# Lookup gates of the expert layer: two groups of four tokens in one run, in a fixed order between the projections

## The chip, the cores and the metric

One core of a Trainium2 chip runs the whole program. The metric is the device time in microseconds of that core, as the median over runs. The core has TensorE (PE in the rows; its weight loads are PEld), VectorE (DVE), ScalarE (ACT), GpSimd (POOL) and SyncE (SP), which issues the loads. Each engine takes its instructions in the order in which the built program lists them, and waits for the others by semaphores.

## The reference, cut to what matters

Two blocks run one after the other on 256 tokens of width 1024. The first has two layers, and each ends with `peer`, a layer that looks up 16 of 16384 experts for each token and head. The change touches that function alone, which runs twice.

```python
def peer(xn, w_q, sub_keys, u, v):
    q = (t @ w_q).reshape(n_tok, PEER_HEADS, 2, PEER_DKEY // 2)
    sc = jnp.einsum('thpd,hpnd->thpn', q, sub_keys).astype(jnp.float32)
    s1, i1 = lax.top_k(sc[:, :, 0], PEER_TOPK)
    s2, i2 = lax.top_k(sc[:, :, 1], PEER_TOPK)
...
    top_s, pos = lax.top_k(cand, PEER_TOPK)
    eidx = jnp.take_along_axis(cidx, pos, axis=-1)
    gate = jax.nn.softmax(top_s, axis=-1).astype(xn.dtype)
...
        hid = jax.nn.gelu(jnp.einsum('td,thkd->thk', tc, u[ec]), approximate=False)
        return jnp.einsum('thk,thkd->td', gc * hid, v[ec])
```

## The kernel before

The kernel does not gather experts. It computes the hidden value of all 128 x 128 experts for all tokens, multiplies it by a gate matrix that is zero where an expert is not picked, and multiplies the product by all of `peer_v`.

**Projections.** The loop over `i1` makes 128 projections, one for each first key. A projection is `acc_t`: 24 matmuls of 128x256 into the PSUM tile `ph`, 16 with the high half `whi` of a block of `peer_u` and 8 with its low half `wlo`. `wload` fetches the block into `raw`; ScalarE casts `whi`, VectorE subtracts to get `wlo` (both L98, two buffers each). ScalarE's Gelu takes `ph` to a row of H, which is three tiles: `low` (rows 0 to 63, H_2056 in the order's rows of the first layer), `mid` (64 to 95, H_1356) and `last` (96 to 127, H_1349). PSUM has two `ph` buffers.

**Routing.** Beside the first projections VectorE runs the list `steps`, which finds the experts of every token; `advance` deals some of it out after each projection. It ends with four lookups (L724 to L731) and `to_picks`, which transposes the picks on TensorE (`it`, L738) and casts them to `IT` (L744, L745). The scratch of these steps lies in `mid` and `last`.

**Gates.** Four tokens are a group, and there are 64 groups. `build` has VectorE make the rows of a group: `pab` (one 128x1024 comparison, L801) and `pgb` (two 128x512 products, L806), in two buffers each. `gates` has TensorE multiply them in 8 half-precision matmuls into the PSUM tile `g`. Then, for the rows of H that exist by then, VectorE multiplies H by `g` (L824), and for the others ScalarE copies `g` there (L826), so that a later Gelu is multiplied in (L842, L843).

**Values.** After the last projection, H is split into two halves `hw` (L98), and 128 blocks of `peer_v` are accumulated into four PSUM tiles `acc`.

**Order.** The program is written with these loops, and a scheduler places each instruction in its engine's list by what it needs. Before, the gates were tied to nothing but their data. The order in which gates and projections stand on TensorE was the scheduler's.

Of the kernel before, what the change touches and what calls it, by code (L numbers as in the profile page):

```python
# [19 lines left out]
P = 128  # L20
S = 256
D = 1024
DK = D // P
# [16 lines left out]
NO_SYNC = mybir.DependencyInfo(mybir.DependencyClass.NoSync, mybir.DependencyReason.DATA)  # L40
# [13 lines left out]
def program(tc, A, out, stop=None, start=None):  # L54
# [22 lines left out]
    def mmt(nm, side=None):  # L77
        banks[0] += 1
        return mm_ps.tile([P, 512], F32, tag=f"mm{banks[0] % 2 if side is None else side}", name=nm)

    def smt(nm="sm"):
        return sm_ps.tile([P, 512], F32, tag="sm", name=nm)
# [19 lines left out]
    def wload(src, pool=None, tag="w", raws=None, rawtag="raw", after=None, behind=None):  # L102
        raw = (raws or rawp).tile([P, 1024], F32, tag=rawtag, name="raw")
        with tc.issue_after(after) if after else nullcontext():
            loads[:] = [nc.sync.dma_start(raw, src)]
        hi = (pool or wp).tile([P, 1024], F32R, tag=tag + "hi", name=tag + "hi")
        lo = (pool or wp).tile([P, 1024], F32R, tag=tag + "lo", name=tag + "lo")
        i = split(raw, hi, lo)
        for x, y in zip(i, behind or ()):
            tc.add_manual_dep(x.ins, y.ins.name, NO_SYNC, reason="behind")  # L110
        return hi, lo
# [5 lines left out]
    def mm(o, l, r, start, stop):  # L117

        i = nc.tensor.matmul(o, l, r, start=start, stop=stop)  # L119
        per, n = paced  # L120
        if per and n // per < len(marks):
            tc.add_manual_dep(i.ins, marks[n // per].name, NO_SYNC, reason="pace")
            paced[1] += 1
        return i
# [6 lines left out]
    def acc_t(o, w, xT, base, nk, n=P):  # L131

        for a, bs in ((0, (0, 1)), (1, (0,))):
            for k in range(nk):
                ws = w[a][:, base + k * P:base + k * P + n]
                for b in bs:
                    mm(o, ws, xT[b][:, k, :], a == 0 and b == 0 and k == 0, a == 1 and k == nk - 1)

    def acc_w(o, w, x, nk, n=P):

# [32 lines left out]
    def proj_t(o, src, xT, n=P):  # L173
        acc_t(o, wload(src), xT, 0, DK, n)
# [45 lines left out]
    def xtiles():  # L220
        both = xp.tile([P, 2, DK, S], F32R, tag="x", name="x")
        x = Parts(both[:, i, :, :] for i in range(2))
        x.both = both
        return x
# [391 lines left out]
    def peer(l, xT, make):  # L616
        with ExitStack() as es:
# [3 lines left out]
            last = hbp.tile([P, 32, S], F32, tag="last", name="H")  # L621
# [47 lines left out]
            def first_level(t, c):  # L669
                def f():  # L670
                    hh, r = divmod(c, 2)
                    top16(SC[:, t, c, :], SV[:, t, hh, r, :], SI[:, t, hh, r, :], tmp)
                return 1.0, f
# [73 lines left out]
            steps = [first_level(t, c) for c in range(16) for t in range(2)]  # L747
# [6 lines left out]
            done = [0]  # L754
            credit = [0.0]

            def advance(limit, us):
                credit[0] = min(credit[0] + us, 4.0)
                while done[0] < min(limit, len(steps)) and credit[0] > 0:
                    cost, f = steps[done[0]]  # L760
                    f()
                    done[0] += 1
                    credit[0] -= cost

            def score(c):
                q = qTs[c % 2]
                ps = smt("sc")
                for t in range(2):
                    mm(ps[:, tok(t)], q[:, tok(t)], keys[:, c * P:(c + 1) * P], True, True)
                ACT.copy(SC[:, :, c, :], ps[:, :S].rearrange("p (t n) -> p t n", t=2))  # L770

            ws = [wload(A["peer_w_q"][l, c]) for c in range(2)]
            pqs = [mmt("pq") for _ in range(2)]
            acc_first(pqs, ws, xT)
            for c in range(16):
                if c > 1:
                    pq = mmt("pq")
                    acc_t(pq[:, :S], w, xT, 0, DK)
                if c > 0:
                    w = wload(A["peer_w_q"][l, c + 1] if c < 15 else A["peer_u"][l, 0])  # L780
                if c > 1:
                    ACT.copy(qTs[c % 2], pq[:, :S])
                else:
                    halves_first(qTs[c], pqs[c])
                if c > 0:
                    score(c - 1)
                advance(2 * c - 2, STEP_US)
# [3 lines left out]
            def rows(a, b):  # L791
                return next(x[:, a - o:b - o, :] for o, end, x in parts if b <= end)

            built = {}

            def build(grp):


                it = IT[:, grp].rearrange("p r t k -> p (r t) k")[:, :, None, :]
                ab = pw.tile([P, 2, 4, P], F16, tag="pab", name="pab", bufs=2)  # L800
                V.tensor_tensor(ab.rearrange("p r t (i k) -> p (r t) i k", k=2),  # L801
                                iota1.rearrange("p (i k) -> p i k", k=2)[:, None, :, :].to_broadcast([P, 8, 64, 2]),
                                it[:, 0:8].to_broadcast([P, 8, 64, 2]), op=ALU.is_equal)
                g = pw.tile([P, 4, 2, P], F16, tag="pgb", name="pgb", bufs=2)
                for r in range(2):
                    V.tensor_tensor(g[:, :, r, :].rearrange("p t (i k) -> p t i k", k=2),  # L806
                                    ab[:, 0].rearrange("p t (i k) -> p t i k", k=2),
                                    it[:, 8 + 4 * r:12 + 4 * r].to_broadcast([P, 4, 64, 2]), op=ALU.mult)
                built[grp] = ab, g

            def gates(grp, n):

                t0 = 4 * grp
                ab, g = built.pop(grp)
                ps = smt("g")
                for i in range(4):
                    for r in range(2):
                        mm(ps[:, i * P:(i + 1) * P], ab[:, 1, i, :], g[:, i, r, :], r == 0, r == 1)
                pv = ps.rearrange("p (t i) -> p i t", t=4)
                for o, end, part in parts:  # L820
                    hv = part[:, :, t0:t0 + 4]
                    m = min(max(n, o), end)
                    if m > o:
                        V.tensor_tensor(hv[:, :m - o], hv[:, :m - o], pv[:, o:m], op=ALU.mult)  # L824
                    if m < end:
                        ACT.copy(hv[:, m - o:], pv[:, m:end])  # L826

            grp, due = 0, 0.0
            for i1 in range(NK):
                ph = mmt("ph")  # L830
                acc_t(ph[:, :S], w, xT, 0, DK)
                if i1 < NK - 1:
                    w = wload(A["peer_u"][l, i1 + 1])
                if i1 == 0:
                    score(15)
                tk = 4 * grp
                hrow = rows(i1, i1 + 1)[:, 0, :]
                if tk < S:
                    ACT.activation(hrow[:, tk:], ph[:, tk:S], AF.Gelu)  # L839
                if tk > 0:  # L840
                    ge = pw.tile([P, 512], F32, tag="pw", name="ge")
                    ACT.activation(ge[:, :tk], ph[:, :tk], AF.Gelu)  # L842
                    V.tensor_tensor(hrow[:, :tk], hrow[:, :tk], ge[:, :tk], op=ALU.mult)  # L843
                if done[0] < len(steps):
                    advance(len(steps), STEP_US)
                    rate = 64.0 / (NK - 2 - i1)
                else:
                    due += rate
                    while due >= 1.0 and grp < 64:
                        if grp not in built:  # L850
                            build(grp)
                        gates(grp, i1 + 1)
                        grp += 1
                        due -= 1.0
                    if grp < 64 and grp not in built:
                        build(grp)
            while grp < 64:
                if grp not in built:
                    build(grp)
                gates(grp, NK)  # L860
                grp += 1
# [9 lines left out]
            for i1 in range(0, NK, 2):  # L871
                if i1 == 96:
# [4 lines left out]
                w = [(tail if keep else pw).tile([P, 2, S], F32R, tag=f"w{i}{i1}" if keep else "pw", name="hw")  # L877
                     for i in range(2)]
# [801 lines left out]
    else:  # L1680
        xT = xtiles()
        to_T(lambda t, k: h[:, t, k * P:(k + 1) * P], DK, lambda k, ps: split(ps, xT[0][:, k, :], xT[1][:, k, :]))
        if origin != "ln0":
# [10 lines left out]
            xT = (xT, pre, xn) if origin == "ln1" else (xT, pp, {}, ExitStack())  # L1694
# [127 lines left out]
```

## Time and profile before

| | |
|---|---|
| median of 3 runs | 2553.38 us (2549.7 to 2555.8) |
| the profiled execution | 2553.41 us, its span 2551.6 us |
| TensorE busy over the span | 2482.0 us, 97% |
| VectorE, ScalarE busy | 1894.3 us (74%), 1347.0 us (53%) |
| granted TensorE clock, mean over the span | 0.991 |

A busy TensorE counts the time between the start of a matmul and its modelled end, and neighbours overlap, so that a stretch without a gap shows as 100% busy whatever the matmuls in it are. How fast it goes there is read from the starts of the groups.

### The profile page before, as it was taken

The page shows a single profiled execution, that of the slowest core. Times are in us where ns is not written, and L with a number is a line of the kernel's source. Part 1 is how long each engine was busy: PE and PEld are TensorE (multiplying, and loading weights), DVE is VectorE, ACT ScalarE, POOL GpSimd, SP SyncE. Part 2 cuts the span into 40 slices and gives each one's busy share as a digit, 9 for nine tenths or more (in the row PEclk, how much of TensorE's full clock was granted, in tenths as well). Part 3 has the DMA queues.
Part 4 walks back from the last instruction along what each step waited for, and adds up shares of the span by engine and source line. Part 5 has one row for each costly group of instructions (what it writes and reads, how often), then busy time and mean ns, then how long its engine had stood idle before and what let it go on. Part 6 is the DMA issues. An engine that isn't in the chain of part 4 may idle for free. (4 is left out here: it accounts for less than half of the span.)

```text
span 2551.6 us, 42276 instructions
## 1 busy us (share of the span) xinstructions
PE 2482.0 (97%) x16202; PEld 2230.8 (87%) x16202; DVE 1894.3 (74%) x3669; ACT 1347.0 (53%) x2316; POOL 3.2 (0%) x24
## 2 busy tenths in 40 slices
PE   8999999999999999999999999999989999899997
PEld 7889999998888879899999998888878899688885
DVE  6679987886555567799878875555567567799997
ACT  5645555444444544556555444445464424488882
POOL 0000000000000000000000000000000000000000
PEclk9999999999999999999999999999999999999998
DMA  6535554455555554555545555556634214699993
GB/s 209 172 119 179 174 163 164 165 165 174 194 194 192 195 190 166 175 167 181 165 165 166 166 165 193 194 192 220 200 126 135 83 51 164 231 344 349 348 338 108
DMA packets 131779, 474.76 MB, mean 186 GB/s; under 512 B 15218, under 2 KB 16242, under 8 KB 131314
## 3 DMA queue, kind: packets, MB, share of 16 engines
q1 hardware_dynamic: 131570, 472.00, 54.7%
q8 instruction: 129, 2.11, 0.4%
q14 instruction: 80, 0.66, 0.1%
HBM read 470.89 MB, written 1.05 MB: 185 GB/s over the span
## 5 line engine op out<-in xcount | busy, mean ns | idle before, releaser
L98 DVE TENSOR_TENSOR wlo<-raw,whi 128x1024 fp32r<-128x1024 f32 x740 | 904.5, 1224 | 465.2 <-ACT whi L98 424.9
L98 ACT CAST whi<-raw 128x1024 fp32r<-128x1024 f32 x740 | 776.4, 1051 | 833.0 <-PE acc L119 332.6
L119 PE MATMUL ph<-x,whi 128*128 128x256 f32 x4096 | 542.5, 285 | 0.0
L119 PEld LDWEIGHTS ph<-x,whi 128*128 128x128 f32 x4096 | 508.2, 191 | 0.0
L119 PE MATMUL acc<-whi,hw 128*128 128x512 f32 x1952 | 483.7, 389 | 2.5 <-ACT hw L98 2.2
L119 PEld LDWEIGHTS acc<-whi,hw 128*128 128x128 f32 x1952 | 366.1, 188 | 79.7 <-ACT hw L98 2.6
L119 PE MATMUL ph<-x,wlo 128*128 128x256 f32 x2048 | 291.0, 284 | 0.0
L119 PEld LDWEIGHTS ph<-x,wlo 128*128 128x128 f32 x2048 | 265.4, 192 | 0.0
L119 PE MATMUL acc<-wlo,hw 128*128 128x512 f32 x976 | 261.5, 389 | 0.0
L119 PEld LDWEIGHTS acc<-wlo,hw 128*128 128x128 f32 x976 | 183.3, 188 | 38.1
L98 DVE TENSOR_TENSOR mlo<-raw,mhi 128x1024 fp32r<-128x1024 f32 x96 | 117.2, 1224 | 11.2 <-ACT mhi L98 8.3
L98 ACT CAST mhi<-raw 128x1024 fp32r<-128x1024 f32 x96 | 100.8, 1051 | 26.9 <-PE gu L119 19.7
L806 DVE TENSOR_TENSOR pgb<-pab,IT 128x512 f16<-128x512 f16 x256 | 97.0, 422 | 1.9
L839 ACT ACTIVATE H<-ph 128x256 f32<-128x256 f32 (+40 forms) x254 | 77.4, 305 | 27.3 <-PE ph L119 27.1
L801 DVE TENSOR_TENSOR pab<-iota,IT 128x1024 f16<-128x1024 f16 x128 | 87.7, 687 | 0.0
L826 ACT COPY H<-g 128x128 f32<-128x128 f32 (+20 forms) x254 | 48.2, 244 | 73.9 <-DVE H L824 73.8
L98 DVE TENSOR_TENSOR hw<-H,hw 128x512 fp32r<-128x512 f32 x128 | 87.1, 684 | 0.0
L824 DVE TENSOR_TENSOR H<-H,g 128x256 f32<-128x256 f32 (+26 forms) x254 | 71.6, 316 | 12.4 <-PE g L119 12.3
L119 PE MATMUL g<-pgb,pab 128*128 128x128 f16 x1024 | 80.8, 220 | 0.0
L98 ACT CAST hw<-H 128x512 fp32r<-128x512 f32 x128 | 77.8, 613 | 0.0
L119 PE MATMUL pq<-x,whi 128*128 128x256 f32 x512 | 73.8, 293 | 4.1 <-DVE x L302 3.2
L119 PE MATMUL gu<-whi,xc 128*128 128x512 f32 x256 | 72.6, 402 | 0.0
(635 smaller groups left out, 3121.8 us busy)
## 6 DMA issues: line engine op xcount, KB each, us to landing
raw<-in_peer_u SPq DMA_DIRECT2D x256, 512.0 KB, 3.3
raw<-in_peer_v SPq DMA_DIRECT2D x256, 512.0 KB, 4.2
raw<-in_exp_gu SPq DMA_DIRECT2D x128, 512.0 KB, 5.4
raw<-in_exp_down SPq DMA_DIRECT2D x64, 512.0 KB, 5.3
raw<-in_peer_w_q SPq DMA_DIRECT2D x32, 512.0 KB, 3.3
raw<-in_even_w_in SPq DMA_DIRECT2D x28, 512.0 KB, 4.3
raw<-in_odd_w_in SPq DMA_DIRECT2D x24, 512.0 KB, 3.4
raw<-in_w_in_g SPq DMA_DIRECT2D x16, 512.0 KB, 3.4
```

The lines of the kernel that those rows point to most:

```text
L98: return ACT.copy(hi, src), V.tensor_tensor(lo, src, hi, op=ALU.subtract)
L119: i = nc.tensor.matmul(o, l, r, start=start, stop=stop)
L801: V.tensor_tensor(ab.rearrange("p r t (i k) -> p (r t) i k", k=2), iota1.rearrange("p (i k) -> p i k", k=2)[:, None, :, :].to_broadcast([P ...
L806: V.tensor_tensor(g[:, :, r, :].rearrange("p t (i k) -> p t i k", k=2), ab[:, 0].rearrange("p t (i k) -> p t i k", k=2), it[:, 8 + 4 * r:1 ...
L824: V.tensor_tensor(hv[:, :m - o], hv[:, :m - o], pv[:, o:m], op=ALU.mult)
L826: ACT.copy(hv[:, m - o:], pv[:, m:end])
L839: ACT.activation(hrow[:, tk:], ph[:, tk:S], AF.Gelu)
```

## The change

`acc_t` returns its first and last matmul. Once the routing has ended, a chain of scheduling orders (they cost no instruction) ties each projection's last matmul, the gate matmuls that the code has behind it, and the next projection's first matmul, one behind the other. Gates are dealt out two groups at a time, whenever two are due, and after every projection the rows of the next two groups are built if they aren't yet.

```diff
@@ acc_t
-                    mm(o, ws, xT[b][:, k, :], a == 0 and b == 0 and k == 0, a == 1 and k == nk - 1)
+                    i = mm(o, ws, xT[b][:, k, :], a == 0 and b == 0 and k == 0, a == 1 and k == nk - 1)
+                    if a == 0 and b == 0 and k == 0:
+                        first = i
+        return first, i
@@ gates
+            last = [None]
...
-                        mm(ps[:, i * P:(i + 1) * P], ab[:, 1, i, :], g[:, i, r, :], r == 0, r == 1)
+                        m = mm(ps[:, i * P:(i + 1) * P], ab[:, 1, i, :], g[:, i, r, :], r == 0, r == 1)
+                        if last[0] is not None:
+                            tc.add_manual_dep(m.ins, last[0].ins.name, NO_SYNC, reason="in turn")
+                        last[0] = m
@@ the loop over i1
-                acc_t(ph[:, :S], w, xT, 0, DK)
+                i = acc_t(ph[:, :S], w, xT, 0, DK)
+                if last[0] is not None:
+                    tc.add_manual_dep(i[0].ins, last[0].ins.name, NO_SYNC, reason="in turn")
+                last[0] = i[1] if done[0] == len(steps) else None
...
-                    while due >= 1.0 and grp < 64:
-                        if grp not in built:
-                            build(grp)
-                        gates(grp, i1 + 1)
-                        grp += 1
-                        due -= 1.0
-                    if grp < 64 and grp not in built:
-                        build(grp)
+
+                    if due >= 2.0:
+                        for g in range(grp, min(grp + 2, 64)):
+                            if g not in built:
+                                build(g)
+                            gates(g, i1 + 1)
+                        grp = min(grp + 2, 64)
+                        due -= 2.0
+                    for g in range(grp, min(grp + 2, 64)):
+                        if g not in built:
+                            build(g)
```

The lines below the first edit stand 3 lower in the changed file, those below the second 9, 12 or 15 lower: L738 is L741 there, L801 is L804, L806 is L809, L824 is L833 and L843 is L855.

**TensorE, the first gates of the first layer.** `it_3205` and `it_3213` are the transposed picks of the two halves of the tokens, `ph_...` are projections in turn. Before:

```order
L119 MATMUL ph_3308<-x_1078,wlo_3286 128x256 x8
L119 MATMUL ph_3343<-x_1078,whi_3335 128x256 x16
L119 MATMUL ph_3343<-x_1078,wlo_3336 128x256 x8
L119 MATMUL ph_3396<-x_1078,whi_3370 128x256 x9
L738 MATMUL it_3205<-ident_82,H_1349 128x128 x2
L119 MATMUL ph_3396<-x_1078,whi_3370 128x256 x7
L119 MATMUL ph_3396<-x_1078,wlo_3371 128x256 x8
L119 MATMUL ph_3449<-x_1078,whi_3423 128x256 x16
L119 MATMUL ph_3484<-x_1078,whi_3476 128x256 x16
L119 MATMUL ph_3449<-x_1078,wlo_3424 128x256 x8
```

Now:

```order
L119 MATMUL ph_3295<-x_1078,wlo_3291 128x256 x8
L119 MATMUL ph_3327<-x_1078,whi_3322 128x256 x16
L119 MATMUL ph_3327<-x_1078,wlo_3323 128x256 x8
L741 MATMUL it_3205<-ident_82,H_1349 128x128 x2
L741 MATMUL it_3213<-ident_82,H_1349 128x128
L119 LDWEIGHTS pab_3253
L119 MATMUL g_3359<-pgb_3255,pab_3253 128x128
...
L119 MATMUL g_3372<-pgb_3260,pab_3258 128x128
L119 MATMUL ph_3395<-x_1078,whi_3354 128x256 x16
```

Before, 95 further projection matmuls stood between the two transposes of `it_3205` and the first gate matmul. Now the 16 matmuls of groups 0 and 1 stand right behind the transposes from which their rows are made, and the next projection stands behind all of them. From there on a run of 16 follows each third projection, up to the last run.

**VectorE, the same place.** The names are those of the routing's last steps and of the rows of groups 0 and 1. Before:

```order
L744 CAST IT_1350<-it_3205 128x32x8 x3
L98 TENSOR_TENSOR wlo_3424<-raw_3421,whi_3423 128x1024
L726 TENSOR_TENSOR H_1349<-H_1349 128x2048
L731 TENSOR_TENSOR H_1349<-H_1349 128x128
L801 TENSOR_TENSOR pab_3253<-iota1_1351,IT_1350 128x1024
L801 TENSOR_TENSOR pab_3303<-iota1_1351,IT_1350 128x1024
L98 TENSOR_TENSOR wlo_3477<-raw_3474,whi_3476 128x1024
L745 TENSOR_TENSOR IT_1350<-it_3205,IT_1350 128x32x8
L729 TENSOR_TENSOR H_1349<-H_1349 128x1024
L806 TENSOR_TENSOR pgb_3255<-pab_3253,IT_1350 128x4x128
L806 TENSOR_TENSOR pgb_3305<-pab_3303,IT_1350 128x4x128
L98 TENSOR_TENSOR wlo_3512<-raw_3509,whi_3511 128x1024
```

Now, without a row left out:

```order
L747 CAST IT_1350<-it_3205 128x32x8 x3
L732 TENSOR_TENSOR H_1349<-H_1349 128x512
L727 TENSOR_TENSOR H_1349<-H_1349 128x2048
L804 TENSOR_TENSOR pab_3253<-iota1_1351,IT_1350 128x1024
L804 TENSOR_TENSOR pab_3258<-iota1_1351,IT_1350 128x1024
L98 TENSOR_TENSOR wlo_3423<-raw_3420,whi_3422 128x1024
L748 TENSOR_TENSOR IT_1350<-it_3205,IT_1350 128x32x8
L732 TENSOR_TENSOR H_1349<-H_1349 128x256
L729 TENSOR_TENSOR H_1349<-H_1349 128x2048
L809 TENSOR_TENSOR pgb_3255<-pab_3253,IT_1350 128x4x128
L809 TENSOR_TENSOR pgb_3260<-pab_3258,IT_1350 128x4x128
L809 TENSOR_TENSOR pgb_3255<-pab_3253,IT_1350 128x4x128
```

The casts of `IT` moved ahead of the last lookups, and the rows of groups 0 and 1 still stand behind three lookup steps, a `wlo` and each other. The second layer has the same rows in the same order on both engines.

**VectorE, the end of the projections.** Before, the last gates stood one projection earlier, and only a `wlo` and one product stood ahead of the first `hw`:

```order
L824 TENSOR_TENSOR H_1349<-H_1349,g_7747 128x31x4
L843 TENSOR_TENSOR H_1349<-H_1349,ge_7744 128x252
L98 TENSOR_TENSOR wlo_7805<-raw_7802,whi_7804 128x1024
L843 TENSOR_TENSOR H_1349<-H_1349,ge_7785 128x256
L98 TENSOR_TENSOR hw_7793<-H_2056,hw_7792 128x512
```

Now the last two groups (`g_7757` and `g_7769`) come after the last projection:

```order
L98 TENSOR_TENSOR wlo_7798<-raw_7795,whi_7797 128x1024
L833 TENSOR_TENSOR H_2056<-H_2056,g_7757 128x64x4
L833 TENSOR_TENSOR H_1356<-H_1356,g_7757 128x32x4
L855 TENSOR_TENSOR H_1349<-H_1349,ge_7754 128x248
L833 TENSOR_TENSOR H_1349<-H_1349,g_7757 128x32x4
L833 TENSOR_TENSOR H_2056<-H_2056,g_7769 128x64x4
L833 TENSOR_TENSOR H_1356<-H_1356,g_7769 128x32x4
L833 TENSOR_TENSOR H_1349<-H_1349,g_7769 128x32x4
L98 TENSOR_TENSOR hw_7786<-H_2056,hw_7785 128x512
```

Five more products moved between the last `wlo` and the first `hw`, whose cast on ScalarE reads what the sixth of these rows writes, `H_2056` times `g_7769`.

## Rows read from the trace of the kernel before

**Rows 1.** Windows: busy time and instructions of each engine, granted clock, loads.

```profile
core 0: us, PE busy (x) PEld busy (x) DVE busy (x) ACT busy (x) POOL busy (x), PEclk, DMA share, GB/s
300.00:600.00 300.00, 300.00 (x2745) 297.10 (x2744) 249.57 (x520) 150.05 (x405) 0.00 (x0) 1.00 0.50 164
```

**Rows 2.** Timeline of PE amid the projections: start, length, operation, count.

```profile
401.07 1.12 PE L119 MATMUL ph<-x,wlo 128*128 128x256 f32 x8
...
403.95 1.12 PE L119 MATMUL ph<-x,wlo 128*128 128x256 f32 x8
404.91 0.62 PE L119 MATMUL g<-pgb,pab 128*128 128x128 f16 x8
...
407.33 1.12 PE L119 MATMUL ph<-x,wlo 128*128 128x256 f32 x8
```

**Rows 3.** Timeline of PE, gates in pieces of 1 and 15.

```profile
333.61 0.23 PE L119 MATMUL g<-pgb,pab 128*128 128x128 f16 x1
333.65 0.48 PE L119 MATMUL ph<-x,wlo 128*128 128x256 f32 x2
333.97 1.01 PE L119 MATMUL g<-pgb,pab 128*128 128x128 f16 x15
```

**Rows 4.** Timeline of PE where the first layer's picks are transposed.

```profile
296.52 1.12 PE L119 MATMUL ph<-x,wlo 128*128 128x256 f32 x8
...
298.56 0.38 PE L738 MATMUL it<-ident,H 128*128 128x128 f32 x2
```

**Rows 5.** Timeline of DVE from there to the first gate rows.

```profile
296.21 1.15 DVE L729 TENSOR_TENSOR H<-H 128x1024 bf16<-128x1024 bf16 x2
...
298.98 1.09 DVE L744 CAST IT<-it 128x256 f16<-128x256 f32 x3 [0.29 <-PE it L738]
299.98 1.22 DVE L98 TENSOR_TENSOR wlo<-raw,whi 128x1024 fp32r<-128x1024 f32 x1
301.12 1.22 DVE L726 TENSOR_TENSOR H<-H 128x2048 bf16<-128x2048 bf16 x1
302.25 0.29 DVE L731 TENSOR_TENSOR H<-H 128x128 f32<-128x128 bf16 x1
302.45 1.29 DVE L801 TENSOR_TENSOR pab<-iota,IT 128x1024 f16<-128x1024 f16 x2
303.66 1.22 DVE L98 TENSOR_TENSOR wlo<-raw,whi 128x1024 fp32r<-128x1024 f32 x1
304.79 0.42 DVE L745 TENSOR_TENSOR IT<-it,IT 128x256 f16<-128x256 f32 x1
305.12 0.68 DVE L729 TENSOR_TENSOR H<-H 128x1024 bf16<-128x1024 bf16 x1
305.72 0.76 DVE L806 TENSOR_TENSOR pgb<-pab,IT 128x512 f16<-128x512 f16 x2
306.39 1.22 DVE L98 TENSOR_TENSOR wlo<-raw,whi 128x1024 fp32r<-128x1024 f32 x1
```

**Rows 6.** Timelines of PE and of DVE, the same place in the second layer.

```profile
1206.04 1.12 PE L119 MATMUL ph<-x,wlo 128*128 128x256 f32 x8
...
1205.73 1.15 DVE L729 TENSOR_TENSOR H<-H 128x1024 bf16<-128x1024 bf16 x2
```

**Rows 7.** Timelines of DVE, ACT and PE, end of the first layer's projections.

```profile
599.17 0.81 DVE L824 TENSOR_TENSOR H<-H,g 128x256 f32<-128x256 f32 x3
599.89 0.41 DVE L843 TENSOR_TENSOR H<-H,ge 128x252 f32<-128x252 f32 x1
601.46 1.23 DVE L98 TENSOR_TENSOR wlo<-raw,whi 128x1024 fp32r<-128x1024 f32 x1 [1.15 <-ACT whi L98]
...
601.65 1.14 ACT L98 CAST hw<-H 128x512 fp32r<-128x512 f32 x2
...
600.13 1.12 PE L119 MATMUL ph<-x,wlo 128*128 128x256 f32 x8
602.33 2.08 PE L119 MATMUL acc<-whi,hw 128*128 128x512 f32 x6 [1.08 <-ACT hw L98]
```

**Rows 8.** Windows around two stretches at the lower clock: columns as in the first group.

```profile
147.20:151.26 4.06, 4.06 (x20) 4.06 (x20) 0.16 (x2) 2.11 (x3) 0.00 (x0) 0.50 0.00 0
...
2509.13:2513.54 4.41, 0.00 (x0) 0.03 (x1) 4.20 (x16) 0.00 (x0) 0.00 (x0) 1.00 0.73 258
2513.54:2520.36 6.82, 6.41 (x18) 4.92 (x19) 6.64 (x20) 5.41 (x7) 0.00 (x0) 0.50 0.04 13
```

## The prediction

> **What bounds the kernel now.** I read the windows first, to see which engine sets the pace of the stage that the change touches. In 300 us of the projections TensorE is busy for all 300.00, at granted clock 1.00, VectorE for 249.57 (83%) and ScalarE for half [rows 1]. The reader is to see that TensorE has no gap there: nothing can be won by removing a wait, only by making TensorE's own list shorter, and each microsecond in which it stands still is lost in full.
>
> The timeline of TensorE tells what could be shorter. Two `wlo` groups of neighbouring projections start 403.95 - 401.07 = 2.88 us apart without gates between them and 407.33 - 403.95 = 3.38 us apart with a run of 8 [rows 2]: the run costs 0.50 us. A run of 15 lasts 1.01 us against 0.62 for 8 [rows 2, 3], so a further gate matmul costs 0.39/7 = 0.056 us, and 8 of them 0.45. The other 0.05 us are the price of going over to gates and back.
>
> Then I looked for the place where the fixed order ties TensorE to an engine that is late. That is the end of the routing, where VectorE alone runs the lookups. I laid the new list of VectorE over the timeline of the old one.
>
> **The change part by part.**
>
> *Fewer runs.* In the built order gates stand in 68 pieces in each layer before and in 32 runs of 16 now. 36 changes less at 0.05 us save 1.8 us in a layer. From below I take 1.4 (0.04 each), from above 2.4 (0.067 each, if the pieces of 1 and 7 cost more than a whole run). The matmuls themselves are the same.
>
> *The first run.* This is the largest term. Up to the transposes both lists are equal, and so is the time: the last projection ahead of the new first run is the one whose `wlo` matmuls start at 296.52 [rows 4], 8 at 0.12 us, so that it ends at 297.48. The two transposes of the first half follow. Before, the casts of `IT` began 298.98 - 298.56 = 0.42 us after their transposes [rows 4, 5]; now they begin at 297.48 + 0.42 = 297.90. VectorE is there in time: it started its 1024-wide lookup step at 296.21, and that is done by 297. From 297.90 on it has this list, each priced by the distance to the next start in rows 5: three `IT` casts 1.00, the 512-wide step 0.34 (as the L745 of the same length, 304.79 to 305.12), a 2048-wide step 1.13 (301.12 to 302.25), two `pab` 1.21, a `wlo` 1.13, L745 0.33, a 256-wide step 0.20 (302.25 to 302.45, same busy time), a 2048-wide step 1.13, two `pgb` 0.67 and the third `pgb` at its full 0.42. The sum is 7.56, and it ends at 305.46 [rows 5].
>
> The first gate matmul needs the first `pgb`, the second the third. TensorE has its three transposes issued by 297.81 and can do nothing but wait until 305.5, for behind the 16 gate matmuls stands the next projection, tied by the change. Before, 95 projection matmuls covered the same time. The wait is 7.7 us. ScalarE, with its `whi` casts and Gelus, and the loads on SyncE are ahead then; neither is what is waited for. The second layer has the same lists, and its `wlo` group and lookup step stand 0.31 us apart (1206.04, 1205.73) as in the first (296.52, 296.21) [rows 4, 5, 6], so it waits for the same 7.7. My bounds are 7.0 (the unhidden ends shorter) and 8.2.
>
> *What the wait does to the clock.* No row shows TensorE idle for 7.7 us amid dense work. [...]
>
> *Behind the first run.* Where does the delay go next? Rows for the second run are ready early: once the three remaining lookup steps are done VectorE has two products, two `pab`, four `pgb` and three casts, some 7 us of work, while TensorE needs 9 us for 16 gates and three projections. ScalarE's six copies of `g` wait until the lookups' scratch in `last` is free and then hold a `whi` and a Gelu behind them; laid out by the same rows they come a few tenths of a microsecond ahead of need.
>
> *The steady cycle.* Three projections and a run last 3 x 2.88 + 0.05 + 16 x 0.056 = 9.6 us. VectorE in that time has three `wlo` (3.4), two `pab` (1.21), four `pgb` (1.34), the products of two groups (about 1.4) and three products L843 (at most 1.2), 8.6 us in all. Its order puts the rows of the next run right behind the products of the last one, so they stand some 4 us behind a run and are wanted 8.6 us behind it. Behind them in VectorE's queue is a `wlo` which is wanted 2 us later than it gets done. I cost this at nothing; without that slack each of 30 runs would wait.
>
> *The end of the projections.* Before, `acc` began at 602.33, 1.24 us after the last projection was issued (600.13 + 8 x 0.12 = 601.09) [rows 7]. Now the 16 gates (0.95 us) stand between, and the first `hw` waits for products queued behind a `wlo` that still starts at 601.46 [rows 7]: done at 602.60, then the five rows up to `H_2056` times `g_7769`. Three products of a group take 599.89 - 599.17 = 0.72, one of 256 wide 0.33, the last at its full 0.41: 602.60 + 0.72 + 0.33 + 0.41 = 604.06, and `acc` follows a cast's start by 602.33 - 601.65 = 0.68: 604.8. That is 2.45 us later, of which 0.95 are gates that went from earlier; 1.5 is lost, less some 0.3 because the low half of `hw` is then not waited for. I take 1.2, with 0.8 and 1.6 as bounds.
>
> **The sum.** In a layer -1.8 + 7.7 + 1.5 + 1.2 = +8.6; in two, +17.2 us. On the profiled execution's 2553.41 (its span is 2551.6) that is 2570.6, and since the median is 2553.38 I forecast 2570.5. The bounds added up: -2.4 + 7.0 + 0 + 0.8 = 5.4 and -1.4 + 8.2 + 3.0 + 1.6 = 11.4 in a layer, so 2564 to 2576.
>
> **The rivals.** 0.2%, about what a measurement of this kernel can tell from no change, is 5.1 us.
>
> *The first run does not wait* (the other side). If the rows of groups 0 and 1 were ready when TensorE comes to them, -1.8 + 1.2 in a layer would remain: 2552.2, no change, or 2549.8 if the end costs nothing either. It decides this way if the third `pgb` is done before 297.8 instead of 305.5. Against it is the list of VectorE, in which three `IT` casts that need the transposes stand ahead of it. [...] Chance 0.05.
>
> *The wait is half covered.* If VectorE's lookup steps behind the transposes ran earlier than my overlay has it, and the wait were some 3 us with no drop of the clock: -1.8 + 3 + 1.2 = +2.4 in a layer, 2558.2, within 0.2%. Chance 0.05.
>
> *Steady runs wait too.* If each of the other 31 runs waited 0.3 us, for a `pgb` or for a `whi` held behind ScalarE's copies, 2 x 9.3 = 18.6 us come on top: 2589. VectorE's 83% speaks for it, the slack above against it. Chance 0.08.
>
> *The forecast*, a wait of seven to eight microseconds in each layer with or without a drop of the clock: 0.82.
>
> **How the numbers follow.** The likeliest case has 2564 to 2576. I give 2560 to 2578, to take in part of the half covered wait and a small wait in the steady runs. Slower by over 0.2%: the forecast, the steady waits and little of the rest, 0.90. Within 0.2%: 0.07. Faster: 0.03.
>
> **What would show it.** In the changed kernel's timeline of TensorE a gap of 7 to 8 us ahead of the first `g` of each layer, ended by a `pgb` of VectorE, and the granted clock at 0.50 around its end. Behind it 16 gate matmuls that cost about 0.95 us in every cycle of 9.6, and no gap between them. At the end of the projections an idle time of 2.5 to 2.8 us ahead of `acc` instead of 1.08. I am wrong if the first gap is under 3 us, if gaps stand ahead of later runs, or if a cycle comes out much shorter than 9.6.

## The result, and the profile after

| | before | after |
|---|---|---|
| median | 2551.47 us (2549.7 to 2555.8, 5 runs) | 2579.34 us (2574.95 to 2581.38, 5 runs) |
| the profiled execution, its span | 2553.41 us, 2551.6 us | 2581.38 us, 2579.6 us |
| mean granted clock | 0.991 | 0.984 |

The ratio is 1.0106, 95% interval 1.0095 to 1.0117: 27.9 us or 1.1% slower. The forecast was 2570.5 us with a range from 2560 to 2578, and 2579.34 lies 1.3 us above the range. The sign came as forecast, and TensorE waits where the forecast said, but the size was 60% above it.

TensorE's timeline at the first gates of the first layer shows the wait. The columns are start, length, engine, line, operation, count, and in brackets the idle time before it and what ended it.

```profile
295.20 1.12 PE L119 MATMUL ph<-x,wlo 128*128 128x256 f32 x8
296.16 0.38 PE L741 MATMUL it<-ident,H 128*128 128x128 f32 x2
304.83 0.45 PE L741 MATMUL it<-ident,H 128*128 128x128 f32 x1 [8.29 <-DVE H L734]
305.07 1.91 PE L119 MATMUL g<-pgb,pab 128*128 128x128 f16 x16
306.75 3.76 PE L119 MATMUL ph<-x,whi 128*128 128x256 f32 x16
310.31 0.71 PE L119 MATMUL ph<-x,wlo 128*128 128x256 f32 x4
...
316.35 1.12 PE L119 MATMUL ph<-x,wlo 128*128 128x256 f32 x8
317.31 1.07 PE L119 MATMUL g<-pgb,pab 128*128 128x128 f16 x16
```

The third row is the one to look at: what stands still is not a gate but the third transpose of the picks (`it`), and what ends its wait is a lookup step (L734), not a `pgb`. The first projection behind the gates takes nearly twice its time, 3.56 us for 16 matmuls from 306.75 to the next start at 310.31, where 16 take 1.92 elsewhere. The second layer repeats it:

```profile
1229.73 0.45 PE L741 MATMUL it<-ident,H 128*128 128x128 f32 x1 [8.29 <-DVE H L734]
```

VectorE's timeline over the same wait, in the order of the list that the prediction priced from [rows 5]:

```profile
296.58 1.08 DVE L747 CAST IT<-it 128x256 f16<-128x256 f32 x3 [1.01 <-PE it L741]
297.58 0.41 DVE L732 TENSOR_TENSOR H<-H 128x512 bf16<-128x512 bf16 x1
297.92 1.22 DVE L727 TENSOR_TENSOR H<-H 128x2048 bf16<-128x2048 bf16 x1
299.05 1.28 DVE L804 TENSOR_TENSOR pab<-iota,IT 128x1024 f16<-128x1024 f16 x2
300.26 1.22 DVE L98 TENSOR_TENSOR wlo<-raw,whi 128x1024 fp32r<-128x1024 f32 x1
301.39 0.41 DVE L748 TENSOR_TENSOR IT<-it,IT 128x256 f16<-128x256 f32 x1
301.73 0.28 DVE L732 TENSOR_TENSOR H<-H 128x256 bf16<-128x256 bf16 x1
301.93 1.21 DVE L729 TENSOR_TENSOR H<-H 128x2048 bf16<-128x2048 bf16 x1
303.06 1.42 DVE L809 TENSOR_TENSOR pgb<-pab,IT 128x512 f16<-128x512 f16 x4
304.40 0.28 DVE L734 TENSOR_TENSOR H<-H 128x128 f32<-128x128 bf16 x1
```

All engines are 1.32 us earlier here than before (197.62 against 198.94 at the first projection), so that the forecast time of 305.46 for the third `pgb` reads 304.14. It came at 304.15: 303.06 plus two starts of 0.335 and a length of 0.42. But L734 stands behind the fourth, and TensorE needs it first.

The windows give the granted clock in the seventh figure behind the stretch (PEclk), ahead of the share of the loads:

```profile
296.38:304.83 8.45, 0.16 (x2) 0.03 (x1) 8.25 (x17) 0.50 (x2) 0.00 (x0) 0.73 0.33 117
304.83:310.45 5.62, 5.62 (x34) 5.56 (x35) 4.42 (x12) 1.19 (x6) 0.00 (x0) 0.50 0.01 3
310.50:606.00 295.50, 295.50 (x2709) 294.21 (x2708) 234.35 (x489) 149.12 (x397) 0.00 (x0) 1.00 0.50 164
611.42:617.70 6.28, 6.28 (x15) 4.93 (x16) 1.80 (x3) 1.51 (x2) 0.00 (x0) 0.50 0.10 38
972.63:976.04 3.41, 3.41 (x19) 3.41 (x18) 0.42 (x1) 2.29 (x3) 0.00 (x0) 0.50 0.02 5
```

They stand for: the wait, in which the clock falls (1.00 in the 3.83 us up to 300.21, 0.50 in the 4.62 after that); 5.62 us of dense work at half clock (0.50) behind it; the steady cycle, 295.50 us without a gap and at full clock (1.00); 6.28 us at half clock behind the end of the projections; and one of two short drops between the layers (3.41 us at 0.50), at places that the change does not touch.

The end of the first layer's projections on VectorE, ScalarE and TensorE, to be held against [rows 7]:

```profile
608.11 1.23 DVE L98 TENSOR_TENSOR wlo<-raw,whi 128x1024 fp32r<-128x1024 f32 x1 [1.33 <-ACT whi L98]
609.25 0.61 DVE L833 TENSOR_TENSOR H<-H,g 128x256 f32<-128x256 f32 x2
609.78 0.41 DVE L855 TENSOR_TENSOR H<-H,ge 128x248 f32<-128x248 f32 x1
610.11 1.00 DVE L833 TENSOR_TENSOR H<-H,g 128x128 f32<-128x128 f32 x4
...
610.75 1.14 ACT L98 CAST hw<-H 128x512 fp32r<-128x512 f32 x2 [2.31 <-DVE H L833]
...
606.83 1.12 PE L119 MATMUL ph<-x,wlo 128*128 128x256 f32 x8
607.79 1.07 PE L119 MATMUL g<-pgb,pab 128*128 128x128 f16 x16
611.42 2.93 PE L119 MATMUL acc<-whi,hw 128*128 128x512 f32 x6 [2.56 <-ACT hw L98]
```

From the last `wlo` group to `acc` it is 4.59 us now and was 2.20; 0.95 of the difference are the gates, 1.44 are lost.

**Where the 28 us lie.** The starts of the first projection and of the first and last `acc` cut the span into stretches. Their lengths in the profiled executions, with those of the experiments below (us; "rest" is all ahead of the first layer's stage, and what is behind the second's values up to TensorE's last instruction; the 10.45 us after that are the same in every run):

| kernel | stage 1 | values 1 | between | stage 2 | values 2 | rest |
|---|---|---|---|---|---|---|
| before | 403.38 | 350.00 | 156.15 | 403.38 | 348.71 | 879.6 |
| after | 413.80 | 351.95 | 159.15 | 413.85 | 349.46 | 880.9 |
| after, second profile (e11) | 413.73 | 349.01 | 159.22 | 413.56 | 348.23 | 881.4 |
| e1, first run untied | 408.70 | 350.57 | 159.16 | 410.19 | 348.25 | 883.0 |
| e2, last run earlier | 412.30 | 349.44 | 156.19 | 412.42 | 348.56 | 882.3 |
| the same again (e12) | 412.38 | 349.38 | 156.19 | 412.50 | 348.63 | 877.8 |
| e3, picks in halves | 411.89 | 350.69 | 159.16 | 411.82 | 349.67 | 879.2 |
| e4, wait filled | 410.75 | 349.01 | 159.08 | 410.75 | 348.20 | 881.2 |
| e5, later, and last run earlier | 401.44 | 349.40 | 157.67 | 401.46 | 348.51 | 880.2 |
| e6, later alone | 402.76 | 350.55 | 157.69 | 402.78 | 349.64 | 875.0 |
| e7, order, one group | 416.52 | 349.41 | 156.14 | 416.30 | 348.52 | 883.0 |
| e8, pairs without order | 405.36 | 350.75 | 159.21 | 405.36 | 349.70 | 882.2 |
| e9, 57 more matmuls | 410.03 | 349.43 | 159.12 | 410.04 | 348.53 | 878.9 |
| e10, 71 more matmuls | 411.87 | 349.42 | 157.60 | 411.84 | 348.62 | 878.1 |

In the changed kernel 10.42 + 10.47 = 20.9 us are lost in the two stages, 2.7 in the values behind them, 3.0 between the layers and 1.4 in the rest. The sum that the prediction made, 17.2 us, was one over the stages alone.

### The profile page after: what moved, and what is told of

The parts are those of the page before. It is cut to its first block, busy times and chain, and to the rows that moved or that the text cites. A ratio compares the mean times of both kernels' runs of the same rounds, so it can differ in the third digit from the quotient of the medians.

```text
span 2579.6 us, 42259 instructions
## 1 busy us (share of the span) xinstructions
PE 2490.7 (97%) x16202; PEld 2241.3 (87%) x16202; DVE 1887.4 (73%) x3667; ACT 1348.1 (52%) x2308; POOL 3.2 (0%) x24
## 5 line engine op out<-in xcount | busy, mean ns | idle before, releaser
L809 DVE TENSOR_TENSOR pgb<-pab,IT 128x512 f16<-128x512 f16 x256 | 93.7, 415 | 0.0
L804 DVE TENSOR_TENSOR pab<-iota,IT 128x1024 f16<-128x1024 f16 x128 | 87.2, 682 | 0.0
L851 ACT ACTIVATE H<-ph 128x256 f32<-128x256 f32 (+31 forms) x256 | 78.3, 306 | 10.9 <-PE ph L119 10.8
L119 PE MATMUL gu<-mhi,xc 128*128 128x512 f32 x256 | 72.3, 401 | 0.0
L833 DVE TENSOR_TENSOR H<-H,g 128x256 f32<-128x256 f32 (+21 forms) x256 | 71.4, 313 | 0.3 <-PE g L119 0.3
```

## The experiments

**The first run without its ties (e1).** The projection ahead of the first pair and the one behind it are not tied; all later ones are.

```diff
-                last[0] = i[1] if done[0] == len(steps) else None
+                last[0] = i[1] if done[0] == len(steps) and grp > 0 else None
@@ behind the first pair's gates
+                        if grp == 0:
+                            last[0] = None
```

> The first run of 16 gates of each layer is left out of the chain of orders; all else is as in the changed kernel. Theory A (the time went into TensorE's wait ahead of the first run, 8.4 us, and the half clock behind it, 2.5 us, in each layer): TensorE now has 63 further projection matmuls between the picks' transposes and the first gates, no wait there, 22 us less than the changed kernel, about 2557, and a stage that is shorter than before by 2 us less 1.4 us at its end. Rival B (the fixed order costs time all along, and the first wait would only be handed on to later runs): little less than the changed kernel, 2570 or more, with gaps ahead of later runs.

2569.14 us (2567.93 to 2572.13) on 2551.69, ratio 1.0065 [1.0052, 1.0079]. 10 us of the 28 came back, less than half of what was expected to. TensorE's timeline shows why. The scheduler moved the first pair's gates to the place right ahead of the second pair's, which are still tied. 63 projection matmuls now stand between the transposes and the first gates. These still wait for `pgb`, 0.75 and 0.44 us, and the transposes between the two pairs wait 2.83 us for a lookup step:

```profile
306.36 0.23 PE L119 MATMUL g<-pgb,pab 128*128 128x128 f16 x1 [0.75 <-DVE pgb L809]
307.02 1.00 PE L119 MATMUL g<-pgb,pab 128*128 128x128 f16 x15 [0.44 <-DVE pgb L809]
310.85 0.69 PE L741 MATMUL it<-ident,H 128*128 128x128 f32 x2 [2.83 <-DVE H L734]
311.33 2.00 PE L119 MATMUL g<-pgb,pab 128*128 128x128 f16 x16
```

63 matmuls cover 63 x 0.12 = 7.6 us, and VectorE's list up to the fourth `pgb` took 9.3 us (298.00 to 307.30 there). So the rival of the expectation, a wait that is handed on to a later run, held for the larger part of what was still waited, 2.83 of 4.02 us in this layer. A scheduler that is free does not make a place safe: the list has to be priced against its cover here too.

**The picks in two halves (e3).** The second half of the tokens is transposed behind the first pair's gates, so that no transpose stands between the first half's and the gates.

```diff
-            def to_picks():
-                for t in range(2):
+            def to_picks(ts=(0,)):
+                for t in ts:
@@ behind the first pair's gates
+                        if grp == 0:
+                            to_picks((1,))
```

> The picks of the second half of the tokens are transposed behind the first run instead of ahead of it; VectorE's list up to the third gate-weighted row is the same. If the first run waits for its rows alone, as predicted, nothing changes: a wait of 8.4 us. If it waited for the transpose that stands ahead of it, which needs a lookup step behind the four products of the rows, the wait falls to about 7.7 us and ends with a product of VectorE, and the kernel is about 1.5 us faster than the changed one.

2574.93 us (2571.5 to 2581.84) on 2551.69, ratio 1.0094 [1.0078, 1.011]. The interval overlaps that of the changed kernel, so the stages decide. A `pgb` now ends the wait, as the prediction had it, and the stages are 1.9 and 2.0 us shorter than in the changed kernel:

```profile
305.40 0.29 PE L119 MATMUL g<-pgb,pab 128*128 128x128 f16 x1 [6.99 <-DVE pgb L809]
306.07 1.76 PE L119 MATMUL g<-pgb,pab 128*128 128x128 f16 x15 [0.38 <-DVE pgb L809]
```

6.99 and 0.38 against 8.29 us: the second half's transpose lengthened the wait by 0.9 us. The other 1.1 us go with the clock, which is at 0.50 for 6.8 us here (from 302.22) and for 10.2 us in the changed kernel (from 300.21).

**The wait filled with work (e4).** As e3, with 60 more matmuls of a projection's size ahead of the first gates, written to the gates' PSUM tile, where the gates overwrite them. The scheduler puts 9 of the 60 ahead of the transposes and 51 behind them.

```diff
+                if grp == 0:
+                    for j in range(60):
+                        m = mm(ps[:, :S], xT[0][:, 0, :P], xT[0][:, j % DK, :], True, True)
...
```

> As the kernel with the picks in halves, with 60 more projection-sized matmuls ahead of the first run in each layer, into the gates' PSUM tile, which the first gate matmul overwrites; they end 7.2 us behind the last projection, so that TensorE is busy for most of the wait and the rows come little later than without them. Theory A's second half (the wait brings the drop of the clock, and that costs 2.5 us in each layer): the granted clock stays at 1.00 behind the first run and the kernel is 3 to 5 us faster than the one with the picks in halves, although TensorE does 14 us more work. Rival (the clock has another cause, or the slow matmuls behind the first run cost nothing): the same time or up to 2 us slower.

2571.87 us (2569.11 to 2573.45) on 2551.69, ratio 1.0076 [1.0062, 1.009]. 14.4 us more of matmuls (120 x 0.12) made each stage 1.1 us shorter than in e3, and the median 3.1 us (the intervals of the two ratios overlap; the stages decide). Around the first run no moment is below full clock, and TensorE's 22.53 busy us of 23.00 leave little but one wait of 0.45:

```profile
295.00:318.00 23.00, 22.53 (x204) 22.24 (x203) 20.51 (x42) 9.59 (x20) 0.00 (x0) 1.00 0.35 115
```

The trace has no drop in the rest of either stage; the nearest starts at 968.03, between the layers. The gates stand in e3 as in e4. With 7.37 us idle ahead of them the clock was at 0.50 for 6.8 us, with 0.45 us it stayed at 1.00. So the clock's fall at the first run went with the idle time here, not with the gates.

**The first pair later (e5, e6).** The dealing starts four groups in arrears and runs a little faster, so that the first pair comes when its rows are made. e5 also has the edit of e2.

```diff
-                    rate = 64.0 / (NK - 2 - i1)
+                    rate, due = 68.0 / (NK - 2 - i1), -4.0
```

> The changed kernel with its first run dealt out six projections later (due starts at -4) and its last run ahead of the last projection; all runs stay tied. VectorE's list from the picks' transposes to the third product of the rows is priced at 9.8 us by its rows in the kernel with the first run untied, and 111 projection matmuls, 13.3 us, now cover it. Theory A (the loss is the wait at the first run, the one at the end, and the half clock that they bring; the runs of 16 themselves save 2 us a layer): no gap of TensorE in either stage, the clock at 1.00 in both, 4 us less than the kernel before, about 2547.5. Rival B (a fixed order of runs costs more than these two waits): at or above the kernel before, 2551 or more.

> As the kernel with both, but with the last run behind the last projection as in the changed kernel. Theory A: 1.4 us of waiting at the end of each layer, less some 0.3 us behind it, and a drop of the clock in those executions in which it comes: 2 to 7 us slower than the kernel with both, 2550 to 2554. If the end costs nothing, the same as that kernel.

e5: 2550.78 us (2547.17 to 2555.19, 11 runs) on 2552.26, ratio 0.9994 [0.9985, 1.0004]. e6: 2550.67 us (2545.87 to 2556.36, 11 runs), ratio 0.9993 [0.9984, 1.0002]. The wait is gone. e6, which has no other edit, is 28.7 us under the changed kernel, 22.1 of them in the two stages: 2 x 11.0, which is what the wait and the half clock behind it cost (worked out below). In e5's timeline of TensorE the first run of 16 stands 111 projection matmuls behind the first transposes, with nothing in brackets:

```profile
311.61 1.12 PE L119 MATMUL ph<-x,wlo 128*128 128x256 f32 x8
312.57 1.07 PE L119 MATMUL g<-pgb,pab 128*128 128x128 f16 x16
...
600.76 1.19 PE L119 MATMUL acc<-whi,hw 128*128 128x512 f32 x4 [1.08 <-ACT hw L98]
```

Its stages are 1.94 and 1.92 us shorter than before's: that is what the order in pairs gives when nothing waits. In the whole time 3.9 us should show; it measures as no change, with 1.5 us more between the layers in the profile. e6 keeps the wait at the end:

```profile
602.23 2.87 PE L119 MATMUL acc<-whi,hw 128*128 128x512 f32 x6 [2.56 <-ACT hw L98]
```

Its stages are 1.3 us longer than e5's and its values 1.1, 4.9 us in all, yet its median is the same: its rest is 5.2 us shorter. The expectation that e6 would be 2 to 7 us slower failed on this, and what shortened the rest stays open.

**The order, one group at a time (e7), and pairs without the order (e8).** e7 has the chain with before's dealing; e8 deals in pairs, and no chain ties them:

```diff
@@ e8
-                        if last[0] is not None:
-                            tc.add_manual_dep(m.ins, last[0].ins.name, NO_SYNC, reason="in turn")
-                        last[0] = m
...
-                last[0] = i[1] if done[0] == len(steps) else None
```

> The chain of orders alone, with the dealing of before: one group at a time, rows made one group ahead. The first run is due two projections earlier than in the changed kernel, so that TensorE comes to it at 290.6 us in the first layer; by the durations of VectorE's rows its third product is done at about 302.8. Theory A: a wait of about 12 us in each layer and 2 to 3 us of half clock behind it, nearly nothing saved by fewer pieces (64 instead of 68), no run behind the last projection: 26 to 30 us slower than the kernel before, about 2580. Rival (the pairs, not the order, bring the wait): near the kernel before.

> The dealing by two groups alone, without the chain: the scheduler puts 67 pieces between the projections of a layer, as many as before, and eleven gate matmuls stand behind the last projection. Theory A: no wait at the first gates, nothing saved, 1 to 3 us lost at the ends: 2552 to 2557. Rival (the dealing by pairs brings the loss): 2570 or more.

e7: 2579.83 us (2576.01 to 2582.14, 4 runs) on 2552.26, ratio 1.0101 [1.0086, 1.0117], the time that was expected. There are 64 runs of 8 in a layer. Two waits stand ahead of them; with two of 0.4 us behind these they make 9.8 us, where 12 were expected:

```profile
296.57 0.69 PE L741 MATMUL it<-ident,H 128*128 128x128 f32 x2 [3.32 <-DVE H L734]
302.93 0.45 PE L741 MATMUL it<-ident,H 128*128 128x128 f32 x1 [5.67 <-DVE H L734]
```

e8: 2562.81 us (2558.66 to 2564.84, 6 runs), ratio 1.0034 [1.0022, 1.0046], 6 us more than the most that was expected. It has no wait at the first gates. Without the chain the scheduler breaks the pairs up into 67 pieces, so that nothing is saved (60 projections with their gates, from the 61st on, take 192.73 us before, 192.73 in e7, 192.75 in e8 and 191.73 in the changed kernel). Its last gates let `acc` wait 2.90 us, 1.8 more than before: the stages are 2.0 us longer. At half clock for part of what follows it loses another 0.75 and 1.0:

```profile
602.45:608.73 6.28, 6.28 (x20) 5.02 (x21) 2.50 (x3) 1.51 (x2) 0.00 (x0) 0.73 0.16 65
```

So the chain brings the first wait with either dealing, and the saving needs both the chain and the pairs.

**The last run a projection earlier (e2, e12).** In the changed kernel the last pair missed its due time by rounding and went behind the loop, and so behind the last projection.

```diff
-                    if due >= 2.0:
+                    if due >= 2.0 - 1e-6:
```

> Two groups count as due at 2.0 less a millionth, so that the last run stands ahead of the last projection, as the last gates did before, instead of behind it; the first run stays tied. Theory C (the last run behind the last projection costs 1.4 us of waiting, and a drop of the clock that the wait brings costs up to 2.5 us behind it, in each layer): TensorE's idle time ahead of the first value matmul is back at 1.1 us, the granted clock there stays at 1.00, and the kernel is 5 to 6 us faster than the changed one, about 2574. Rival (the drop of the clock at that place is chance and not brought by the wait): 3 us faster at most, 2576, with the clock at 0.50 there all the same.

2569.17 us (2568.74 to 2573.41) on 2551.69, ratio 1.0069 [1.0055, 1.0082]: 10 us under the changed kernel, twice what was expected. TensorE's timeline has the short wait of before:

```profile
611.43 0.73 PE L119 MATMUL acc<-whi,hw 128*128 128x512 f32 x2 [1.08 <-ACT hw L98]
```

Its stages are 1.5 and 1.4 us shorter, its values 2.5 and 0.9, and 3.0 us between the layers are gone. Since a good part of this lies behind the place of the edit, the two kernels were compared once more on one chip (e11, e12):

> The changed kernel once more, on one chip with the run after it. 2579 us on 2552, ratio 1.0105. If the drops near 970 and 1070 us belong to this kernel, its second profile shows them again; if they fall by chance, it shows others or none.

> The changed kernel with its last run of gates ahead of the last projections, once more. If its 10 us under the changed kernel recur on one chip: 2569 us, 10 under the run before it, of which its two stages explain 3 us and the missing drops behind their ends 3 more. If the rest was chance: 2573 us, 6 under it.

The changed kernel: 2579.81 us (2577.39 to 2588.69) on 2553.44, ratio 1.0112 [1.0094, 1.0129]. The last run earlier: 2570.39 us (2569.17 to 2572.93), ratio 1.007 [1.0056, 1.0084]. The 9.4 us recur. The profiles are worth a close look. In e11 the 2.56 us ahead of `acc` brought no drop at all (first row), but the drops between the layers are there again (second row); in e12 that whole stretch is at full clock, as in e2 (third row):

```profile
613.05:619.33 6.28, 6.28 (x27) 5.18 (x28) 2.51 (x3) 2.40 (x3) 0.00 (x0) 1.00 0.13 45
...
970.78:974.18 3.40, 3.40 (x17) 3.40 (x18) 0.20 (x1) 1.38 (x2) 0.00 (x0) 0.50 0.02 5
```

```profile
959.52:1115.71 156.19, 149.87 (x1142) 143.11 (x1141) 121.09 (x340) 78.53 (x136) 0.00 (x0) 1.00 0.49 164
```

The drop behind the end falls in one execution and not in another; the 3.0 us between the layers came in both executions of the one kernel and in neither of the other.

**Nothing but a shift in time (e9, e10).** The kernel before with 57 or 71 more matmuls at the first gates of each layer, overwritten by them, so that all that follows only comes later.

```diff
+                if grp == 0:
+                    for j in range(57):
+                        mm(ps[:, :S], xT[0][:, 0, :P], xT[0][:, j % DK, :], True, True)
```

> The kernel before with 57 more matmuls in each layer, of the size of a projection's, ahead of the first group's gates and into their tile, which the gates overwrite; nothing waits for anything new. Added work: 2 x 57 x 0.120 = 13.7 us, so 2565.9 us on 2552.2. If the drops of the clock outside the stages fall by chance, the excess over the added work is within 1.5 us of 0. If they hang on how far the program has moved in time, this run and the one with 71 differ in that excess, by about 3 us.

> The kernel before with 71 more matmuls in each layer at the same place, as many as take the time by which the change moved the first layer's end. Added work: 2 x 71 x 0.120 = 17.0 us, so 2569.3 us on 2552.2. By chance alone: within 1.5 us of that. If the place in time decides, the later program stands here as in the changed kernel: drops at half clock near 970 and 1070 us as there, and about 3 us over the added work.

With 57: 2567.99 us (2565.01 to 2570.8) on 2553.44, ratio 1.0057 [1.0043, 1.0071], 14.6 us for 13.7 of work. With 71: 2570.47 us (2569.75 to 2572.78), ratio 1.007 [1.0057, 1.0084], 17.0 us for 17.0. By the whole time a shift costs its work and no more that is clear of the intervals. By the profiles it does move drops, but the other way round than expected: 57 has both between the layers (the row), 71 one of them.

```profile
965.80:969.25 3.45, 3.45 (x16) 3.45 (x17) 0.34 (x1) 1.25 (x2) 0.00 (x0) 0.51 0.00 0
```

So these drops do not need the change's order: before with a few matmuls more has them too. What decides whether a kernel gets them was not found.

## Why the prediction was right and wrong

**What bounds the kernel** was right. TensorE's idle time was lost in full (the sum below counts all 8.45 us of the wait and comes to 10.5 us in a layer; the stages are 10.42 and 10.47 longer), and the steady cycle has no gap in 295.50 us. It lasts 191.73/20 = 9.59 us against the 9.6 forecast.

**Fewer runs**, -1.8 us in a layer: right. 32 runs stand there, and with the waits away the stage is 1.93 us shorter (e5). In 60 projections from the 61st on 192.73 - 191.73 = 1.0 us is saved, 0.05 for each of the 20 changes that fall away there (40 pieces and 20 runs), as priced.

**The first run**, +7.7: right in place, too small, and what ends it was wrong. The step that failed is "TensorE has its three transposes issued by 297.81". Only two could be issued. The third reads what L734 writes, and that lookup stands behind the four `pgb` on VectorE; the order showed the third transpose ahead of the gates, but it was taken as ready without a look for its writer. 8.45 us passed from the issue of the second transpose (296.38) to the start of the third, above the bound of 8.2. e3 shows the share of it: without that transpose the wait is 0.9 us shorter. From the issue of the last transpose ahead of the gates, 298.25, to the second gate at 306.07 it is 7.8 us there, so that the price of VectorE's list was right.

**The clock behind the wait**, +1.5 with the bounds 0 and 3.0: the term was the author's estimate, and no run shows it. In its place the runs showed 2.55 us in a layer. The drop that before's trace has behind an idle 4.41 us [rows 8] lasted 6.82 us, shorter than what came here: 4.62 us at 0.50 within the wait, and 5.62 behind it, 10.2 in all. 295.20 to 316.35 in the timeline holds 72 projection matmuls (8.64 us at 0.12), 16 gates (0.95) and five transposes (0.55), 10.1 us of work, and lasts 21.15. Of the 11.0 us lost 8.45 are the wait, and 2.55 are left for the clock; the bound of 3.0 held. The 5.62 us alone would cost 5.62 x (1 - 1.92/3.56) = 2.6, an estimate from the 16 matmuls that took 3.56 us at 0.50 (from 306.75) and take 1.92 at 1.00. e4, with 0.45 us idle at that place, has no moment below 1.00 there.

**The end of the projections**, +1.2: 1.44 us were lost by the stage, against the 1.5 of its sum (which gives 604.74 where it says 604.8), and the idle time of 2.56 us is the forecast one. The 0.3 that it took off for the low half of `hw` lies behind `acc`: without a drop the values are 0.4 us shorter in both layers (e11 against e12), so that 1.0 us is lost where no drop comes, within the bounds of 0.8 to 1.6. But the sum had no term for the clock here; the step that failed is that it was left at nothing without a reason. Of the twelve ends with 2.56 or 2.57 us idle (the changed kernel twice, e1, e3, e4, e6) seven had 3.4 to 6.8 us at half clock at that place; of the fourteen with 1.07 or 1.08 (before, e2, e5, e7, e9, e10, e12) none had. In the profile after the values are 2.7 us longer than before in the two layers together, in its second profile 1.5 us shorter.

**The sum.** In a layer -1.93 + 8.45 + 2.55 + 1.44 = 10.5 us (the stages show 10.42 and 10.47), against 8.6 forecast: 3.7 of the 10.7 us between the forecast's 17.2 and the measured 27.9. The other 7 lie outside the stages, by the profile after 2.7 in the values, 3.0 between the layers and 1.4 in the rest. The first two go with drops of the clock (6.28 us at 0.50 and 3.60 us at a mean of 0.60 behind the two ends, two of 3.41 us at 0.50 between the layers); what made the 1.4 is not shown. The prediction had no term for any of them, and they alone carried the time out of the range: 2553.4 + 20.9 = 2574.3 lies within it. How much lies outside differs from one execution to the next: in the second profile it was 3.4 us.

**The rivals.** The first run did wait, with no half of it covered, and no later run of the changed kernel waited. No projection matmul passed the tied gates: none stands in the 8.29 us of the wait, and the first one behind it starts at 306.75, after the 16 gates (305.07).

**What stays open.** Why the stretch between the layers takes 156.2 us in some profiles, 157.6 in others and 159.2 in half of the fourteen. The length goes with the number of drops of 3.41 us in it, none, one or two. It recurred in the two kernels that were profiled twice, it is not the change's order (e9), and neither the length of the stages nor the time at which the stretch begins sorts it: it begins at 959.6, 959.5 and 959.6 us in e4, e12 and e10, which have the three different lengths. No version was shown to beat the kernel before: e5, whose stages gain 3.9 us, measures within its interval of no change.

## What to carry to other kernels

An order that ties a dense engine to rows made elsewhere saves a little in each cycle and can lose all of it at the first, when the maker is still late: price the maker's whole list up to that point, look for the writer of each tied instruction and not of the last alone, and let the first come later if it doesn't fit (28.7 us of difference here, for one line). A wait of TensorE can be charged with work at half clock behind it as well (2.55 us behind 8.45 here), and the place where the sum ends should be a few microseconds behind the last edit. An effect of one or two microseconds in a stage is read in the stage; in the whole time it drowned here in drops of the clock elsewhere.

## What was not expected of the hardware

The same idle time does not always have the same price: 2.56 us ahead of `acc` brought a drop of the granted clock to 0.50 in seven of twelve cases, and the same kernel had it in one execution and not in another (after, 6.28 us at 0.50; e11, 6.28 us at 1.00). And matmuls that do nothing can pay: 120 of them, 14.4 us of work put into a wait, took 1.1 us off each stage (e4 against e3), since the 7.37 us of each wait (6.99 and 0.38) were lost anyway and the clock stayed at 1.00.
